# Rotary embedding: from half-batch slabs in nine slots to whole batches in five

## The chip, the core and the metric

The kernel runs on one core of a Trainium2 chip. The metric is the time of one execution on the device, in microseconds (us). Several runs are given by their median. A profile is one execution recorded by the hardware; its span runs from its first to its last instruction, and the time of the same execution lies a little above the span.

Five engines work side by side, each with its own order of instructions: TensorE (PE), VectorE (DVE), ScalarE (ACT), GpSimd (POOL) and SyncE (SP). Here SP issues all loads and ACT issues all stores. Sixteen DMA engines carry both. SBUF is the memory on the core, with 128 partitions; PSUM is the smaller one that TensorE writes to.

## The reference

```python
# x: (8, 2048, 8, 64) float32; cos, sin: (2048, 32) float32
x1 = x[..., :32]
x2 = x[..., 32:]
cos = cos[None, :, None, :]
sin = sin[None, :, None, :]
out1 = x1 * cos - x2 * sin
out2 = x1 * sin + x2 * cos
return np.concatenate([out1, out2], axis=-1)
```

Each row of x (one batch, one position, one head, 64 numbers) is rotated by the angle of its position. x is 33.55 MB, the output as much, each table 0.26 MB: for each number of x that is read and written there are two products and one addition.

## The kernel before

**Tiling.** The 2048 positions of a batch are split over 128 partitions, 16 consecutive ones each. So a partition holds 16 x 512 numbers of a batch: a row of 32 KB. The tables lie in the same way, 16 x 32 numbers (2 KB) per partition. A *slab* is half a batch, 8 positions per partition: 128 rows of 16 KB, 2 MB. There are 16 slabs, first the first halves of all batches, then the second halves. They live in `xpool`, nine slots of 16 KB per partition. The result is written over x in its slot, and stored from there.

**The three ways to rotate.** Work on a slab goes in tiles of 2048 numbers per partition (half a slab, 1 MB); the first slab begins and the last slab ends with smaller ones. `rotate` (from line 121) gives each tile one of three kinds. All three need a product t1 = x * cos and a product t2 = x * sin with the halves swapped, and their sum.

- Kind A, the usual one: GpSimd makes t2 in two instructions (L138, one for each half, the second with `nsin`, the negated table); VectorE makes t1 (L144) and adds (L151).
- Kind B: GpSimd makes t2 and VectorE t1, but TensorE adds them, by multiplying both with an identity matrix into the same PSUM bank (L156, L157), in four groups of 512 columns; ACT copies each group back over x (L158).
- Kind C: VectorE makes both products (L144, L161), TensorE adds them (L172, L173, with the negated identity `neye` for the first half), ACT copies (L176). GpSimd has nothing to do.

Slabs 5 and 10 are a C tile followed by a B tile; everything else is kind A.

**Buffers.** t1 of kind A lies in PSUM, in one slot. t2 of kinds A and B lies in `t2_pool`, three slots of 8 KB per partition. t1 of kinds B and C, and t2 of kind C, lie in `t1s_pool`, three slots of 8 KB under the one tag `t1s`. TensorE's sums go to `o_pool`, two PSUM banks. When a tile takes a slot that another one had, its first write waits until every reader of the earlier tile is done. Per partition SBUF holds 9 x 16 KB of slabs, 3 x 8 of `t1s`, 3 x 8 of `t2`, and 7 KB of tables and identities.

**Order.** `keep(...)` holds instructions of one engine in the order in which the program names them; VectorE's products and additions, ACT's evacuating copies and ACT's stores are held so. Stores run two slabs behind the computation (`LAG = 2`): after the tiles of slab i the kernel names the store of slab i - 2. The load of slab i + 6 is named after that; it takes the slot of slab i - 3 and waits for that slab's store. The last slab and the two before it are stored as early as they can be.

**Start.** ACT issues cos, SP issues 256 KB of x, then sin, then the rest of slab 0 in growing pieces (256 KB, 512 KB, 1 MB), then the slabs 1 to 8. ACT makes `nsin` from sin, then `neye`, and a copy of sin in PSUM; VectorE copies cos to PSUM (L108).

Of the kernel before, what the change touches and what calls it, by code (L numbers as in the profile page):

```python
# [9 lines left out]
@with_exitstack  # L10
def kernel(
    ctx: ExitStack,
    tc: tile.TileContext,
    x: bass.AP,
    cos: bass.AP,
    sin: bass.AP,
    out: bass.AP,
):
    nc = tc.nc
    keep = tc.keep_in_program_order  # L20
    f32 = mybir.dt.float32
    PSUM = bass.MemoryType.PSUM

    B, S, H, D = x.shape
    Dh = D // 2
    P = 128
    HD = H * D
    R = S // P

    SL = 8  # L30
    n_half = R // SL
    SLAB = SL * HD
    UNIT = 4 * HD
    NBUF = 9
    C = 512

    xv = x.rearrange("b (q r) h d -> b q (r h d)", q=P)
    ov = out.rearrange("b (q r) h d -> b q (r h d)", q=P)
    cos_src = cos.rearrange("(q r) d -> q r d", q=P)
    sin_src = sin.rearrange("(q r) d -> q r d", q=P)  # L40

    const_pool = ctx.enter_context(tc.tile_pool(name="const", bufs=1))
    tab_pool = ctx.enter_context(tc.tile_pool(name="tab", bufs=1, space=PSUM))
    t1_pool = ctx.enter_context(tc.tile_pool(name="t1p", bufs=1, space=PSUM))
    o_pool = ctx.enter_context(tc.tile_pool(name="op", bufs=2, space=PSUM))
    t1s_pool = ctx.enter_context(tc.tile_pool(name="t1s", bufs=3))
    xpool = ctx.enter_context(tc.tile_pool(name="xpool", bufs=NBUF))
    t2_pool = ctx.enter_context(tc.tile_pool(name="t2p", bufs=3))

    cos_sb = const_pool.tile([P, R, Dh], f32, tag="cb")  # L50
    sin_sb = const_pool.tile([P, R, Dh], f32, tag="sb")
    nsin = const_pool.tile([P, R, Dh], f32, tag="ns")
    eye = const_pool.tile([P, P], f32, tag="eye")
    neye = const_pool.tile([P, P], f32, tag="neye")
    cos_ps = tab_pool.tile([P, R, Dh], f32, tag="cp")
    sin_ps = tab_pool.tile([P, R, Dh], f32, tag="sp")

    slabs = [(b, l) for l in range(n_half) for b in range(B)]
    last = len(slabs) - 1
    xts = {}  # L60

    def cuts(i):
        if i == 0:
            return [HD, HD, 2 * HD, UNIT]
        return [SLAB]

    def pieces(i):
        if i == 0:
            return [HD, HD, 2 * HD, UNIT]
        if i == last:  # L70
            return [UNIT, 2 * HD, HD, HD]
        return [UNIT, UNIT]

    def spans(sizes):
        lo = 0
        for n in sizes:
            yield lo, n
            lo += n

    def load(i):  # L80
        b, l = slabs[i]
        xt = xpool.tile([P, SLAB], f32, tag="xt", name=f"xt{i}")
        for lo, n in spans(cuts(i)):
            nc.sync.dma_start(
                out=xt[:, lo : lo + n],
                in_=xv[b, :, l * SLAB + lo : l * SLAB + lo + n],
            )
            if i == 0 and lo == 0:
                nc.sync.dma_start(out=sin_sb, in_=sin_src)
        xts[i] = xt  # L90

    nc.scalar.dma_start(out=cos_sb, in_=cos_src)
    for i in range(NBUF):
        load(i)

    nc.gpsimd.memset(eye, 0.0)  # L96
    nc.gpsimd.affine_select(
        out=eye,
        in_=eye,
        compare_op=mybir.AluOpType.not_equal,  # L100
        fill=1.0,
        base=0,
        pattern=[[-1, P]],
        channel_multiplier=1,
    )
    nc.scalar.mul(nsin, sin_sb, -1.0)  # L106
    nc.scalar.mul(neye, eye, -1.0)
    nc.vector.tensor_copy(cos_ps, cos_sb)  # L108
    nc.scalar.copy(sin_ps, sin_sb)  # L109

    def rep(a, n):
        return dataclasses.replace(a, ap=[a.ap[0][:], a.ap[1][:], [0, n], a.ap[-1][:]])

    kinds = {}
    for i in (5, 10):
        kinds |= {(i, 0): "C", (i, UNIT): "B"}

    def rotate(i, lo, n):
        b, l = slabs[i]
        kind = kinds.get((i, lo), "A")  # L120
        xt = xts[i][:, lo : lo + n]
        r0 = l * SL + lo // HD
        nr = n // HD
        xk = xt.rearrange("p (r k d) -> p r k d", r=nr, d=Dh)
        xu = xt.rearrange("p (g u d) -> p g u d", u=2, d=Dh)
        if kind == "A":
            t1 = t1_pool.tile([P, n], f32, tag="t1")
        else:
            t1 = t1s_pool.tile([P, n], f32, tag="t1s")
        if kind == "C":  # L130
            t2 = t1s_pool.tile([P, n], f32, tag="t1s")
        else:
            t2 = t2_pool.tile([P, n], f32, tag="t2")
        t1u = t1.rearrange("p (g u d) -> p g u d", u=2, d=Dh)
        t2u = t2.rearrange("p (g u d) -> p g u d", u=2, d=Dh)
        if kind != "C":
            for u, tab in ((1, sin_sb), (0, nsin)):
                nc.gpsimd.tensor_mul(  # L138
                    out=t2u[:, :, u, :].rearrange("p (r h) d -> p r h d", h=H),
                    in0=xu[:, :, 1 - u, :].rearrange("p (r h) d -> p r h d", h=H),  # L140
                    in1=rep(tab[:, r0 : r0 + nr, :], H),
                )
        keep(
            nc.vector.tensor_mul(  # L144
                out=t1.rearrange("p (r k d) -> p r k d", r=nr, d=Dh),
                in0=xk,
                in1=rep(cos_ps[:, r0 : r0 + nr, :], 2 * H),
            )
        )
        if kind == "A":  # L150
            keep(nc.vector.tensor_add(out=xt, in0=t1, in1=t2))  # L151
        elif kind == "B":
            for j in range(n // C):
                o = o_pool.tile([P, C], f32, tag="o")
                cs = slice(j * C, (j + 1) * C)
                nc.tensor.matmul(o, eye, t1[:, cs], start=True, stop=False)  # L156
                nc.tensor.matmul(o, eye, t2[:, cs], start=False, stop=True)  # L157
                keep(nc.scalar.copy(xt[:, cs], o))  # L158
        else:
            keep(  # L160
                nc.vector.tensor_mul(  # L161
                    out=t2.rearrange("p (r k d) -> p r k d", r=nr, d=Dh),
                    in0=xk,
                    in1=rep(sin_ps[:, r0 : r0 + nr, :], 2 * H),
                )
            )
            G = C // Dh
            for u in range(2):
                for j in range(n // 2 // C):
                    o = o_pool.tile([P, C], f32, tag="o")  # L170
                    gs = slice(j * G, (j + 1) * G)
                    nc.tensor.matmul(o, eye, t1u[:, gs, u, :], start=True, stop=False)  # L172
                    nc.tensor.matmul(  # L173
                        o, eye if u else neye, t2u[:, gs, 1 - u, :], start=False, stop=True
                    )
                    keep(nc.scalar.copy(xu[:, gs, u, :], o.rearrange("p (g d) -> p g d", d=Dh)))  # L176

    LAG = 2

    def store(i, lo, n):  # L180
        b, l = slabs[i]
        keep(
            nc.scalar.dma_start(
                out=ov[b, :, l * SLAB + lo : l * SLAB + lo + n],
                in_=xts[i][:, lo : lo + n],
            )
        )

    for i in range(last + 1):
        if i == last:  # L190
            for k in range(i - LAG, i):
                store(k, 0, SLAB)
        for lo, n in spans(pieces(i)):
            rotate(i, lo, n)
            if i == last:
                store(i, lo, n)
        if LAG <= i < last:
            store(i - LAG, 0, SLAB)
        if i > LAG and i - LAG - 1 + NBUF <= last:
            load(i - LAG - 1 + NBUF)  # L200


# [28 lines left out]
```

## Time and profile before

| | |
|---|---|
| median of 3 runs | 164.71 us (164.56 to 164.76) |
| the profiled execution | 164.8 us |
| its span | 163.0 us |
| VectorE busy | 143.4 us (88%), 71 instructions |
| GpSimd busy | 139.4 us (86%), 74 instructions |
| TensorE busy | 33.3 us (20%) |
| ACT busy | 12.0 us (7%) |
| moved by the DMA engines | 67.66 MB |
| L144, tile of 2048 | 30 times, mean 2293 ns |
| L151, tile of 2048 | 26 times, mean 2292 ns |
| L138, 1024 (two per tile of 2048) | 56 times, mean 2336 ns |
| load of a slab, issue to landing | median 27.6 us |
| store of a slab, issue to landing | median 15.3 us |

In the lines of the profile an engine's name is followed by the line of the kernel, the operation, and output <- input. "x2" behind a line of the timeline means that so many instructions were merged. A bracket at the end gives the idle time of the engine just before, and what ended it. In the page's slices each digit stands for a fortieth of the span, 4.1 us, in tenths of busy time. A line of the windows gives, for a stretch of time, the busy time and count of PE, weight loads, DVE, ACT and POOL, then TensorE's granted clock as a share of full speed, the busy share of the DMA engines, and GB/s. A line of the waits names who waited for whom, the total in us, how often, and the longest.

### The profile page before, as it was taken

The numbers are of one execution on the slowest core, as the hardware profiler recorded it, in microseconds if no ns is written. First come the engines' busy times: TensorE is split into PE (matmuls) and PEld (weight loads), VectorE is DVE, ScalarE is ACT, GpSimd is POOL, SyncE is SP. The second block draws the span as 40 slices with busy tenths as digits, with TensorE's granted clock in tenths as the row PEclk, the third lists the DMA queues.
The fourth block names the chain that finished last, engine by engine and source line by source line (L and its number), as shares of the span: only waits on it lengthen the run. The fifth ranks groups of instructions, "written<-read, shape, count | busy, mean of one in ns | idle before, by whom it ended". The sixth has DMA issues, their size and how long they took to land. (4 is left out here: it accounts for less than half of the span.)

```text
span 163.0 us, 480 instructions
## 1 busy us (share of the span) xinstructions
PE 33.3 (20%) x64; PEld 13.4 (8%) x64; DVE 143.4 (88%) x71; ACT 12.0 (7%) x20; POOL 139.4 (86%) x74
## 2 busy tenths in 40 slices
PE   0000000000000079993000000899920000000000
PEld 0000000000000024440000000244400000000000
DVE  0587999999999999999899999999999999999900
ACT  3300000000000002232000000022410000000000
POOL 1599999999999999799999999956999999995000
PEclk9999999999999999999555555579997555555555
DMA  4999999999999999999999999999999999999995
GB/s 137 383 432 442 406 398 426 438 438 418 438 434 426 430 434 430 426 434 438 422 428 438 424 422 446 430 414 446 434 422 430 442 422 422 446 426 430 434 402 207
DMA packets 5763, 67.66 MB, mean 415 GB/s; under 512 B 640, under 2 KB 640, under 8 KB 1664
## 3 DMA queue, kind: packets, MB, share of 16 engines
q1 hardware_dynamic: 2880, 33.82, 49.5%
q10 hardware_dynamic: 2880, 33.82, 48.7%
q14 instruction: 3, 0.02, 0.0%
HBM read 34.08 MB, written 33.55 MB: 415 GB/s over the span
## 5 line engine op out<-in xcount | busy, mean ns | idle before, releaser
L138 POOL TENSOR_TENSOR t<-xt,sin_sb 128x1024 f32<-128x1024 f32 (+2 forms) x34 | 70.7, 2081 | 10.8 <-DVE xt L151 6.3
L144 DVE TENSOR_TENSOR t<-xt,cos_ps 128x2048 f32<-128x2048 f32 (+2 forms) x36 | 73.9, 2056 | 1.0
L138 POOL TENSOR_TENSOR t<-xt,nsin 128x1024 f32<-128x1024 f32 (+2 forms) x34 | 70.8, 2082 | 0.0
L151 DVE TENSOR_TENSOR xt<-t,t 128x2048 f32<-128x2048 f32 (+2 forms) x32 | 64.8, 2025 | 5.6 <-POOL t L138 2.1
L172 PE MATMUL o<-t,eye 128*128 128x512 f32 x16 | 11.3, 800 | 85.8 <-DVE t L144 85.8
L176 ACT COPY xt<-o 128x512 f32<-128x512 f32 x8 | 4.7, 586 | 94.5 <-DVE t L144 55.3
L172 PEld LDWEIGHTS o<-t,eye 128*128 128x128 f32 x16 | 3.9, 256 | 90.6 <-issue 90.6
L156 PE MATMUL o<-t,eye 128*128 128x512 f32 x16 | 8.2, 592 | 0.0
L157 PE MATMUL o<-t,eye 128*128 128x512 f32 x16 | 8.2, 592 | 0.0
L173 PE MATMUL o<-t,neye 128*128 128x512 f32 x8 | 6.2, 862 | 0.2 <-DVE t L161 0.2
L158 ACT COPY xt<-o 128x512 f32<-128x512 f32 x8 | 4.7, 586 | 9.0 <-PE o L157 9.0
L108 DVE COPY cos_ps<-cos_sb 128x512 f32<-128x512 f32 x1 | 0.7, 694 | 5.0 <-DMA cos_sb<-in_cos_dram 5.0
L161 DVE TENSOR_TENSOR t<-xt,sin_ps 128x2048 f32<-128x2048 f32 x2 | 4.6, 2281 | 0.0
L173 PE MATMUL o<-t,eye 128*128 128x512 f32 x8 | 4.1, 592 | 0.0
L157 PEld LDWEIGHTS o<-t,eye 128*128 128x128 f32 x16 | 3.0, 190 | 3.8 <-issue 3.8
L156 PEld LDWEIGHTS o<-t,eye 128*128 128x128 f32 x16 | 3.0, 190 | 3.8 <-issue 3.8
L173 PEld LDWEIGHTS o<-t,neye 128*128 128x128 f32 x8 | 2.0, 278 | 4.9 <-issue 3.3
L173 PEld LDWEIGHTS o<-t,eye 128*128 128x128 f32 x8 | 1.5, 190 | 1.9 <-issue 1.9
L106 ACT ACT_TABLE_LOAD x1 | 1.3, 1283 | 1.2 <-PEq L215 1.2
L106 ACT ACTIVATE nsin<-sin_sb 128x512 f32<-128x512 f32 x1 | 0.6, 630 | 3.2 <-DMA sin_sb<-in_sin_dram 3.2
L109 ACT COPY sin_ps<-sin_sb 128x512 f32<-128x512 f32 x1 | 0.6, 579 | 0.0
L96 POOL MEMSET eye<- 128x128 f32 x1 | 0.2, 205 | 0.3 <-POOLq L215 0.3
(6 smaller groups left out, 1.0 us busy)
## 6 DMA issues: line engine op xcount, KB each, us to landing
xt<-in_x_dram SPq DMA_DIRECT2D x15, 2048.0 KB, 27.6
out_dram<-xt ACTq DMA_DIRECT2D x15, 2048.0 KB, 15.3
xt<-in_x_dram SPq DMA_DIRECT2D x1, 1024.0 KB, 7.8
out_dram<-xt ACTq DMA_DIRECT2D x1, 1024.0 KB, 10.3
xt<-in_x_dram SPq DMA_DIRECT2D x2, 256.0 KB, 4.3
xt<-in_x_dram SPq DMA_DIRECT2D x1, 512.0 KB, 5.8
out_dram<-xt ACTq DMA_DIRECT2D x1, 512.0 KB, 8.9
out_dram<-xt ACTq DMA_DIRECT2D x2, 256.0 KB, 7.6
```

The lines of the kernel that those rows point to most:

```text
L106: nc.scalar.mul(nsin, sin_sb, -1.0)
L108: nc.vector.tensor_copy(cos_ps, cos_sb)
L138: nc.gpsimd.tensor_mul(out=t2u[:, :, u, :].rearrange("p (r h) d -> p r h d", h=H), in0=xu[:, :, 1 - u, :].rearrange("p (r h) d -> p r h d" ...
L144: nc.vector.tensor_mul(out=t1.rearrange("p (r k d) -> p r k d", r=nr, d=Dh), in0=xk, in1=rep(cos_ps[:, r0 : r0 + nr, :], 2 * H),)
L151: keep(nc.vector.tensor_add(out=xt, in0=t1, in1=t2))
L156: nc.tensor.matmul(o, eye, t1[:, cs], start=True, stop=False)
L157: nc.tensor.matmul(o, eye, t2[:, cs], start=False, stop=True)
L158: keep(nc.scalar.copy(xt[:, cs], o))
L161: nc.vector.tensor_mul(out=t2.rearrange("p (r k d) -> p r k d", r=nr, d=Dh), in0=xk, in1=rep(sin_ps[:, r0 : r0 + nr, :], 2 * H),)
L172: nc.tensor.matmul(o, eye, t1u[:, gs, u, :], start=True, stop=False)
L173: nc.tensor.matmul(o, eye if u else neye, t2u[:, gs, 1 - u, :], start=False, stop=True)
L176: keep(nc.scalar.copy(xu[:, gs, u, :], o.rearrange("p (g d) -> p g d", d=Dh)))
```

## The change

- Slabs are gone. A slot of `xpool` holds a whole batch, 128 rows of 32 KB, 4 MB; there are five slots (5 x 32 KB per partition). The eight batches are taken in order, in tiles of 2048 numbers as before: four per batch, the first batch beginning and the last batch ending with two tiles of 1024.
- `t1s_pool` has two slots instead of three.
- SP issues, in this order, the first 1 MB of x, cos, sin, the next 1 MB, the remaining 2 MB of batch 0, and then whole batches. ACT issues no load.
- Each batch is stored as soon as its tiles are named: one store of 4 MB, for the last batch 2 MB, 1 MB and 1 MB. The load of batch b + 5 is named right after the store of batch b.
- TensorE gets five tiles instead of four: batches 1 and 3 begin with a C tile and a B tile, batch 5 with a B tile.
- ACT makes the PSUM copy of sin before `neye`. The preparing instructions, the loads and GpSimd's products are now held in program order too.

```diff
-    NBUF = 9
+    NBUF = 5
...
-    t1s_pool = ctx.enter_context(tc.tile_pool(name="t1s", bufs=3))
+    t1s_pool = ctx.enter_context(tc.tile_pool(name="t1s", bufs=2))
...
+    def load(b):
+        xt = xpool.tile([P, ROW], f32, tag="xt", name=f"xt{b}")
+        for lo, n in spans([UNIT, UNIT, 2 * UNIT] if b == 0 else [ROW]):
+            keep(nc.sync.dma_start(out=xt[:, lo : lo + n], in_=xv[b, :, lo : lo + n]))
+            if b == 0 and lo == 0:
+                keep(nc.sync.dma_start(out=cos_sb, in_=cos_src))
+                keep(nc.sync.dma_start(out=sin_sb, in_=sin_src))
+        xts[b] = xt
+
+    def store(b, lo, n):
+        keep(nc.scalar.dma_start(out=ov[b, :, lo : lo + n], in_=xts[b][:, lo : lo + n]))
+
+    for b in range(NBUF):
+        load(b)
...
-    for i in (5, 10):
-        kinds |= {(i, 0): "C", (i, UNIT): "B"}
+    for b in (1, 3):
+        kinds |= {(b, 0): "C", (b, UNIT): "B"}
+    kinds[(5, 0)] = "B"
...
+    def pieces(b):
+        if b == 0:
+            return [2 * HD, 2 * HD, UNIT, UNIT, UNIT]
+        if b == last:
+            return [UNIT, UNIT, UNIT, 2 * HD, 2 * HD]
+        return [UNIT] * 4
+
+    for b in range(B):
+        done = 0
+        outs = list(spans([2 * UNIT, UNIT, UNIT] if b == last else [ROW]))
+        for lo, n in spans(pieces(b)):
+            rotate(b, lo, n)
+            done = lo + n
+            while outs and sum(outs[0]) <= done:
+                store(b, *outs.pop(0))
+        if b + NBUF <= last:
+            load(b + NBUF)
```

Here `HD` is 512 (one position), `UNIT` is 2048 and `ROW` 8192 numbers per partition. `rotate` itself is unchanged but for its indices and for `keep` around L138.

## The prediction

> **What bounds the kernel now.** I read the page's slices first, then the windows of the quiet stretches, then the timeline around the first pair of TensorE tiles, then the waits. All times in us from the start of the span, unless said otherwise.
>
> ```profile
> DVE  0587999999999999999899999999999999999900
> POOL 1599999999999999799999999956999999995000
> DMA  4999999999999999999999999999999999999995
> ```
>
> The DMA row is full from the second slice to the last but one, so the 16 DMA engines set the end. But VectorE (DVE) is full too, and stops two slices earlier. Two resources lie close together.
>
> ```profile
> 24.00:40.00 16.00, 0.00 (x0) 0.00 (x0) 15.48 (x8) 0.00 (x0) 16.00 (x8) 1.00 1.01 431
> 126.00:150.00 24.00, 0.00 (x0) 0.00 (x0) 23.24 (x11) 0.00 (x0) 22.12 (x13) 0.50 1.01 432
> ```
>
> These are two windows; the last number is GB/s. The engines move 431 GB/s with loads and stores mixed. 67.66 MB at 431 GB/s is 157.0. The last VectorE instruction ends at 154.29 + 0.69 = 155.0, the span at 163.0: 8 us of stores were still queued behind it. So VectorE could be some microseconds later before it counted, and not more.
>
> ```profile
> 57.73 2.28 DVE L161 TENSOR_TENSOR t<-xt,sin_ps 128x2048 f32<-128x2048 f32 x1
> 57.96 2.04 PE L172 MATMUL o<-t,eye 128*128 128x512 f32 x2 [57.96 <-DVE t L144]
> 59.93 4.49 DVE L144 TENSOR_TENSOR t<-xt,cos_ps 128x2048 f32<-128x2048 f32 x2
> 60.16 2.05 PE L173 MATMUL o<-t,neye 128*128 128x512 f32 x2 [0.15 <-DVE t L161]
> ...
> 66.04 1.02 PE L172 MATMUL o<-t,eye 128*128 128x512 f32 x2
> 66.90 1.02 PE L173 MATMUL o<-t,eye 128*128 128x512 f32 x2
> 67.76 1.02 PE L156 MATMUL o<-t,eye 128*128 128x512 f32 x2
> ```
>
> This timeline is what decides my forecast. A kind C tile writes both its products (L144, L161) into slots of `t1s`, and TensorE reads them in four groups, each an L172 and an L173. The last L172 runs from 66.04 to 67.06. VectorE has long gone on: at 59.93, right after L161, it writes the product of the kind B tile into the third slot of `t1s`.
>
> ```profile
> POOL t L138 <- DVE xt L151: 6.3, 3, 3.3
> SPq L84 <- DMA out_dram<-xt: 86.4, 7, 31.9
> ```
>
> The waits show that a writer waits until a slot's readers are done: GpSimd (POOL) for the additions that read its product (three slots), the sync queue for the stores that read an `xt` slot.
>
> **What the Trainium skill says.** "SBUF — State Buffer", section "SBUF size: 192, 224, or 256?", gives about 208 KiB usable per partition. The new kernel takes 5 x 32 for `xt`, 2 x 8 for `t1s`, 3 x 8 for `t2`, 7 for tables and identities: 207 KiB. So the third `t1s` slot has no room; no trace shows the limit itself. "DMA: Bandwidth & Descriptors", section "Queues, rings and completion order", says that an engine takes turns between the queues packet by packet. The trace agrees: with equal rows both ways the queues have 49.5% and 48.7%. I use equal shares below.
>
> **The change, part by part.**
>
> *Two slots in `t1s`.* Batches 1 and 3 begin with a C tile and then a B tile. C holds both slots; B's cosine product must wait for the last L172 (or for L173, 0.86 later). Everything on VectorE is kept in program order, so this wait holds the A tiles behind it too, although they need no `t1s` slot. From the lines above: without a wait B's product starts at 59.93, with it at 67.06 + 0.1 = 67.16: 7.2. At the second pair of the trace the product starts at 104.61 and the last L172 ends at 110.54 + 1.02 = 111.56: 7.05. I take 7.1 each, 14.2 together. Bounds: 6.9 and 8.0 (the L173) each. Below that is excluded as long as the wait is there, since no group can start before C's products are written. The store of the batch on the scalar queue, and the load five batches later behind that, wait too.
>
> *The start.* 1 MB of x and both tables now precede everything in one queue. Before, 0.53 MB moved in the first 4.0 us. The x has 8 KB rows, the tables 2 KB rows (the window 4 to 6, with 2 KB rows, gave 355 GB/s, 6 to 8 399). 1.57 MB then end at 4.0 + 1.04/0.40 = 6.6; before, about 0.85 passed from sin's last byte to its first use: 7.45, where GpSimd started at 5.74. Range 7.0 to 8.0. cos comes 0.65 earlier, so its copy (0.69) is done by 7.5.
>
> *Batch 0.* GpSimd sets it: two pieces of 1024 at 2 x 1.21, three of 2048 at 4.56 (instructions follow each other every 2.28): 7.45 + 4.85 + 13.7 = 26.0; the last addition, 2.3, ends at 28.3.
>
> *Batches 1 to 7 on VectorE.* An A tile takes 4.725 (additions start at 20.25, 24.98, 29.70); a C tile 4.4, a B tile 2.2 (starts at 55.53, 57.73, 59.93). Batches 1 and 3: 4.4 + 7.1 + 2.2 + 9.45 = 23.15. Batches 2, 4, 6: 18.9. Batch 5, with the fifth TensorE tile alone and `t1s` free: 2.2 + 14.2 = 16.4. Batch 7: three A tiles, 14.2, and two halves at 2.6 (149.37 to 151.97): 19.4. Ends: 51.5, 70.4, 93.5, 112.4, 128.8, 147.7, 167.1.
>
> *Does anything else hold it longer?* Loads: read alone till 29.8 (first byte about 2.8), 11.6 MB; then half the rate beside stores. Batch 1 has landed at 24, batch 2 at 41, batch 3 at 60, 4 at 73; load 5 needs store 0 finished (49.5) and lands about 93, load 6 at 109, load 7 at 129. VectorE wants them at 112, 129 and 148. So whole-batch loads cost nothing here, because of the waits; without these see the first rival. GpSimd fills its three `t2` slots during a wait and then keeps ahead at 4.56 a tile; B's slot is read until 6.9 after B's product, which brings the next product exactly in time (0 to 0.5 lost each). ACT evacuates as before and issues store 0 before the C tile's copies: 0.
>
> *The end.* The last store is 1 MB, issued at 167.1 with nothing left in the queues, as a store comes every 4.7 and takes 2.4. Fixed part: the last store of before was issued at 155.0 and took 7.6; after 155 the windows still moved 0.43 + 0.80 + 0.80 + 0.42 = 2.45 MB, 5.7 at 431 GB/s, leaving 1.9 ("DMA: Bandwidth & Descriptors", section "Anatomy of one DMA — SWDGE (gpsimd) path", has about 2.0 for another kind of queue). 1.05/0.431 + 1.9 = 4.35: 171.5. Before, 163.0 - 162.6 = 0.4 followed: a span of about 171.9. Bounds of the tail: 3.7 to 5.5.
>
> *Larger rows, fewer DMAs.* 16 KB rows already give 431 GB/s. If 32 KB rows give up to 1% more, 1.6 us of DMA time is saved; here that is hidden, for VectorE is last.
>
> Sum: 163.0 + 8.9 = 171.9. The profiled run took 164.8, 1.8 more than its span, and lies 0.1 over the median of 164.71. 171.9 + 1.8 - 0.1 = **173.6**.
>
> **Rivals.** *First, the other side: the wait is absent and the DMA engines set the end, 163.6.* Its place is B's product in batches 1 and 3; its price is the DMA engines' own time. Without the 14.2 the work of VectorE would end at 152.9, and then loads hold it: batch 7 would land at 135 (half rate from 29.8 on), so 156.6. The DMA engines need 2.9 + 157.0 + 1.6 = 161.5, and 0.4: a span of 161.9. That saves the slow small rows at both ends and the hole of the window 20 to 22 (319 GB/s). For it: the full DMA row, and 32 KB rows can't be worse than 16 KB by anything seen. Against it: C holds both slots. It decides from this point: the tail behind VectorE is 4.8, so the span stays below 163.0 while VectorE ends before 158.2, that is while the two waits cost under 5.3 together. I work out 14.2. Chance 0.06.
>
> *Second: only one wait counts, 166.5.* If batch 3 came late from HBM, its wait would run in time that VectorE lost anyway. Against it: batch 3 lands at 60 and VectorE reaches it at 70. Chance 0.03.
>
> *Third: the throttle stretches the wait, about 181.* The granted clock falls to 0.5 in the page's slices; were the second C tile's groups at half rate, its wait would be 7 longer. Against it: at a mean clock of 0.81 in the window 100 to 120 the ACT copies still come every 1.72, as in the first pair. Chance 0.04.
>
> **How the numbers follow.** Forecast 0.87, rivals 0.06, 0.03, 0.04. The parts' bounds (waits -0.4 to +1.8, start and batch 0 -0.5 to +0.6, tail -0.6 to +1.1, GpSimd 0 to 1) add up, not all one way, to 171.8 to 176.0; this holds over 9 tenths of the forecast, so about 8 in 10 of all. 0.2% is about what a measurement can tell from no change. Faster: most of the first rival, 0.05; the rest 0.01 within. Slower: 0.94.
>
> **What would show it.** Right: VectorE idle about 7 before L144 in batches 1 and 3, released by L172 of TensorE; no DVE wait on a load after batch 0; batch 0 done near 28; the DMA row no longer full towards the end; VectorE's last end near 167, span near 172. Wrong: DVE busy through both pairs, or waiting on loads of batches 4 to 7, and a DMA row full to the end: then it is the first rival. A first use of the tables far from 7.5, or an A tile other than 4.7, would show a wrong term and move the sum by as much.

## The result, and the profile after

The changed kernel takes 173.55 us (median of 4 runs, 173.02 to 173.9) against 164.72 us before (164.56 to 164.76): a ratio of 1.0535, 95% interval 1.0501 to 1.057. The forecast was 173.6. The profiled execution took 173.02, its span is 171.0.

First the rows of the page's slices for the changed kernel that answer to those of the kernel before. A slice is now 4.3 us.

```profile
DVE  0477999607999999940999999999999999999980
POOL 1399999992099999994049999999999999999700
DMA  5999999999999999999999999999999990598955
```

VectorE has two holes, at slices 8 and 9 and at 18 and 19, where the row before had none. GpSimd has a hole of its own just behind each. The DMA row has its holes somewhere else: it stays full through both of VectorE's and falls to 0 some 60 us after the second.

The chain of work that ended last, by engine:

```profile
DVE 63%; DMA 17%; PE 8%; POOL 6%; issue 3%; SPq 0%; DVEq 0%; ACTq 0%; POOLq 0%
```

Read as shares of the span: the chain runs through VectorE almost from the start, and TensorE (PE) stands in it with 8%. TensorE is busy for a quarter of the span and far from full; it is in the chain only because something on VectorE waited for it. Where, the timeline of VectorE shows. (In the changed kernel the products are L129 for cosine and L146 for sine, the addition is L136, and the matmuls of kind C are L157 and L158.)

```profile
28.27 2.28 DVE L129 TENSOR_TENSOR t<-xt,cos_ps 128x2048 f32<-128x2048 f32 x1
30.47 2.28 DVE L146 TENSOR_TENSOR t<-xt,sin_ps 128x2048 f32<-128x2048 f32 x1
39.69 4.49 DVE L129 TENSOR_TENSOR t<-xt,cos_ps 128x2048 f32<-128x2048 f32 x2 [6.94 <-PE o L157]
44.29 2.29 DVE L136 TENSOR_TENSOR xt<-t,t 128x2048 f32<-128x2048 f32 x1
```

The two products of batch 1's C tile follow each other at 2.20. The next row merges B's product and the first product of the A tile behind it, and its bracket is the new wait: VectorE stood still for 6.94 us, until a matmul of L157 was done. The second pair, from the timeline of both engines:

```profile
72.31 2.28 DVE L146 TENSOR_TENSOR t<-xt,sin_ps 128x2048 f32<-128x2048 f32 x1
...
80.00 1.02 PE L157 MATMUL o<-t,eye 128*128 128x512 f32 x2
80.86 1.02 PE L158 MATMUL o<-t,eye 128*128 128x512 f32 x2
81.06 4.49 DVE L129 TENSOR_TENSOR t<-xt,cos_ps 128x2048 f32<-128x2048 f32 x2 [6.47 <-PE o L157]
```

The last L157 runs from 80.00 to 81.02, and B's product starts at 81.06. It does not wait for the last L158, which starts at 80.86 and is still running. So the slot that B takes is the one of C's cosine product, and it is free as soon as the last reader of that product is done.

At the other end, the windows of the changed kernel (columns as before, the last one GB/s):

```profile
134.00:140.00 6.00, 0.00 (x0) 0.00 (x0) 5.76 (x4) 0.00 (x0) 6.00 (x3) 0.50 1.00 431
140.00:142.00 2.00, 0.00 (x0) 0.00 (x0) 2.00 (x1) 0.00 (x0) 2.00 (x2) 0.50 0.42 180
142.00:146.00 4.00, 0.00 (x0) 0.00 (x0) 3.86 (x3) 0.00 (x0) 4.00 (x3) 0.50 0.00 0
```

Here the price is paid. From 142 to 146 the DMA engines have nothing left: every load has landed, every finished batch is stored, and VectorE is still working on batch 6. Before, VectorE had been ahead and stores were queued behind it until the end.

### The profile page after: what moved, and what is told of

The parts are those of the page before. It is cut to its first block, busy times and chain, and to the rows that moved or that the text cites. A ratio compares the mean times of both kernels' runs of the same rounds, so it can differ in the third digit from the quotient of the medians.

```text
span 171.0 us, 462 instructions
## 1 busy us (share of the span) xinstructions
PE 42.1 (25%) x80; PEld 16.7 (10%) x80; DVE 140.5 (82%) x66; ACT 14.3 (8%) x24; POOL 138.6 (81%) x70
## 2 busy tenths in 40 slices
DMA packets 3170, 67.65 MB, mean 396 GB/s; under 512 B 352, under 2 KB 352, under 8 KB 608
## 4 chain that ended last, share of the span: by engine, by line
DVE 63%; DMA 17%; PE 8%; POOL 6%; issue 3%; SPq 0%; DVEq 0%; ACTq 0%; POOLq 0%
DVE t L129 32%; DVE xt L136 28%; DMA out_dram<-xt 14%; POOL t L122 6%; PE o L158 4%; PE o L157 3%; DMA sin_sb<-in_sin_dram 3%; DVE t L146 3%; DVEq L136 0%; SPq L69 0%; SPq L67 0%; ACTq L74 0%; POOLq L122 0%
## 5 line engine op out<-in xcount | busy, mean ns | idle before, releaser
L122 POOL TENSOR_TENSOR t<-xt,sin_sb 128x1024 f32<-128x1024 f32 (+1 forms) x32 | 70.7, 2211 | 22.4 <-DVE xt L136 16.5
L129 DVE TENSOR_TENSOR t<-xt,cos_ps 128x2048 f32<-128x2048 f32 (+1 forms) x34 | 73.4, 2168 | 14.3 <-PE o L157 13.4
L122 POOL TENSOR_TENSOR t<-xt,nsin 128x1024 f32<-128x1024 f32 (+1 forms) x32 | 70.8, 2211 | 0.0
L136 DVE TENSOR_TENSOR xt<-t,t 128x2048 f32<-128x2048 f32 (+1 forms) x29 | 62.2, 2145 | 5.0 <-POOL t L122 2.2
L157 PE MATMUL o<-t,eye 128*128 128x512 f32 x16 | 10.7, 760 | 54.0 <-DVE t L129 54.0
L141 PE MATMUL o<-t,eye 128*128 128x512 f32 x24 | 13.5, 646 | 26.5 <-DVE t L129 26.5
L142 PE MATMUL o<-t,eye 128*128 128x512 f32 x24 | 13.2, 632 | 0.0
L143 ACT COPY xt<-o 128x512 f32<-128x512 f32 x12 | 7.0, 585 | 42.6 <-PE o L142 42.6
L162 ACT COPY xt<-o 128x512 f32<-128x512 f32 x8 | 4.7, 586 | 60.8 <-PE o L158 60.8
L157 PEld LDWEIGHTS o<-t,eye 128*128 128x128 f32 x16 | 3.8, 251 | 58.8 <-POOL t L122 30.7
L141 PEld LDWEIGHTS o<-t,eye 128*128 128x128 f32 x24 | 4.7, 209 | 33.8 <-issue 29.0
L158 PE MATMUL o<-t,neye 128*128 128x512 f32 x8 | 6.2, 864 | 0.2 <-DVE t L146 0.2
L142 PEld LDWEIGHTS o<-t,eye 128*128 128x128 f32 x24 | 4.9, 203 | 6.3 <-issue 6.3
L146 DVE TENSOR_TENSOR t<-xt,sin_ps 128x2048 f32<-128x2048 f32 x2 | 4.6, 2281 | 0.0
L158 PE MATMUL o<-t,eye 128*128 128x512 f32 x8 | 4.1, 593 | 0.0
L158 PEld LDWEIGHTS o<-t,neye 128*128 128x128 f32 x8 | 1.8, 256 | 4.6 <-issue 2.9
L158 PEld LDWEIGHTS o<-t,eye 128*128 128x128 f32 x8 | 1.5, 190 | 1.9 <-issue 1.9
```

Of the source, the lines that this page charges most:

```text
L122: nc.gpsimd.tensor_mul(out=t2u[:, :, u, :].rearrange("p (r h) d -> p r h d", h=H), in0=xu[:, :, 1 - u, :].rearrange("p (r h) d -> p r h d" ...
L129: nc.vector.tensor_mul(out=t1.rearrange("p (r k d) -> p r k d", r=nr, d=Dh), in0=xk, in1=rep(cos_ps[:, r0 : r0 + nr, :], 2 * H),)
L146: nc.vector.tensor_mul(out=t2.rearrange("p (r k d) -> p r k d", r=nr, d=Dh), in0=xk, in1=rep(sin_ps[:, r0 : r0 + nr, :], 2 * H),)
L158: nc.tensor.matmul(o, eye if u else neye, t2u[:, gs, 1 - u, :], start=False, stop=True)
```

## The experiments

All are timed against the kernel before on the same chip. The first four ask whether the slots of `t1s` make the time, or the coarse batches: one puts the slots alone into the old kernel, one takes the wait away from the new one, one takes half of it away, and one trades it for another wait. The rest ask what sets the end once the wait is gone, and where the 0.6% come from by which the kernel without the wait is faster than the one before.

### 1. The slots alone, in the old kernel

```diff
-    t1s_pool = ctx.enter_context(tc.tile_pool(name="t1s", bufs=3))
+    t1s_pool = ctx.enter_context(tc.tile_pool(name="t1s", bufs=2))
```

> The kernel before with one edit: two t1s slots instead of three. Slot theory: B's cosine product of slabs 5 and 10 waits for the last group of the C tile before it, about 6.9 us each time, twice; VectorE then ends near 155.0 + 13.8 = 168.8, and with the fixed 1.9, the last 256 KB (0.6) and 0.4 behind it the span is about 171.7, the time about 173.5. Rival (whole batches are too coarse: the time is lost by 4 MB loads and stores): nothing of that is in this kernel, so 164.7.

Measured: 172.77, ratio 1.0483 (1.044 to 1.0525). Its waits of VectorE:

```profile
DVE t L144 <- PE o L172: 12.9, 2, 6.5
DVE xt L151 <- POOL t L138: 2.1, 3, 1.0
```

This is the old kernel with its 2 MB slabs, and it loses 8.0 us by one number. Its span is 171.1, as long as that of the changed kernel to 0.1. The second line is the same as before the change. The last VectorE instruction ends at 167.38 + 0.69 = 168.07, 13.1 later than before, which is the 12.9 of the two waits to within 0.2. Whole batches can't be the cause here, for there are none.

### 2. Both pairs apart

Between C and B come the two A tiles of the batch; slots, batches and the number of tiles stay.

```diff
-        kinds |= {(b, 0): "C", (b, UNIT): "B"}
+        kinds |= {(b, 0): "C", (b, 3 * UNIT): "B"}
```

> The changed kernel with the C tile at the head and the B tile at the end of batches 1 and 3, two A tiles between them, so that TensorE is done with C before B's product is due; two slots, whole batches, five tiles stay. Slot theory: no VectorE wait on TensorE; the DMA engines set the end, the first rival's sum: 163.6 (162.5 to 165). VectorE starts to wait for loads from batch 4 on. Coarse-batch rival: still about 173.

Measured: 163.82, ratio 0.9936 (0.9921 to 0.9951): 9.7 us faster than the changed kernel, and 0.6% faster than the one before. The slices:

```profile
DVE  0468899999999999999999999999999999999500
DMA  5999999989999999999999999999999999999995
```

VectorE has no hole, and the DMA row is full to the last slice again. VectorE ends at 151.17 + 1.22 = 152.39, and 9.7 us of stores follow. The time was right, but VectorE's waits for loads, which the expectation named, did not come. Batch 7 was in its slot at 129.4 and not at 135. The sum behind 135 gives the loads half the rate from 29.8 on. In the trace stores move nothing before 32, and again nothing from 52 to 56: store 0 landed at 53.2, and store 1 was issued only at 53.9, because B's evacuation by TensorE and ACT now stands at the end of batch 1. In these 4 us the loads moved 1.74 MB, 0.9 more than at half the rate, which is worth about 4 us to the loads behind. After batch 3 there is no such gap: when store 3 was issued, at 88.3, store 2 was still under way (to 96.5).

### 3. One pair apart

```diff
-    for b in (1, 3):
-        kinds |= {(b, 0): "C", (b, UNIT): "B"}
+    for b, at in ((1, 3 * UNIT), (3, UNIT)):
+        kinds |= {(b, 0): "C", (b, at): "B"}
```

> As the last, but only batch 1 has its pair apart; batch 3 keeps C and B side by side. Slot theory: one wait of about 6.5 is left, VectorE ends near 166.2 - 6.9 = 159.3, then the tail of 4.8: a span near 164.1, time about 166 (165.5 to 167.5). If the two waits do not add (one of them hidden behind late loads), 173 or 163.6. Coarse-batch rival: 173.

Measured: 166.54, ratio 1.0102 (1.007 to 1.0134).

```profile
DVE t L129 <- PE o L157: 6.3, 1, 6.3
```

One wait left, 6.3. From two waits to one the time falls by 7.0; from one to none only by 2.7, because then the DMA engines are last. That bend is what the point of decision in the first rival describes. In the profiled runs VectorE ends at 152.39 without a wait, at 159.21 with one and at 166.16 with two, so 6.8 and 13.8 later, and the span grows by 2.0 and 8.9: some 5 us are free each time, and the rest comes out whole. (The medians, 2.7 and 9.7 above the kernel without a wait, leave a little less free; the kernels with a wait spread more from run to run.)

### 4. Another slot for C's sine product

C's sine product moves to the pool of `t2`, so B finds a free `t1s` slot with the pair side by side.

```diff
-            t2 = t1s_pool.tile([P, n], f32, tag="t1s")
+            t2 = t2_pool.tile([P, n], f32, tag="t2")
```

> The changed kernel with the pair side by side, but C's sine product takes a slot of the t2 pool (three slots) instead of t1s, so that B's cosine product finds a free t1s slot. Slot theory: the wait of VectorE on TensorE before B's product goes; but C now holds a t2 slot until TensorE's fourth group, so GpSimd's second A product of the batch comes later and VectorE's addition waits about 2.6 in each of the two batches. VectorE ends near 166.2 - 2 x (6.7 - 2.6) = 158.0, time near 164.8 (163.6 to 166.5). Coarse-batch rival: 173.

Measured: 168.06, ratio 1.019 (1.0175 to 1.0206), above the expected range. VectorE's waits:

```profile
DVE xt L136 <- POOL t L122: 11.4, 6, 2.4
```

The wait on TensorE is gone, as expected, and additions wait for GpSimd instead. The changed kernel has 2.2 of this in all, at the start; so 9.2 are new, not the 5.2 that I had put in. The expectation counted one addition in each of batches 1 and 3. The timeline shows four: at 44.17 in batch 1, at 81.33 and 88.33 in batch 3, and at 111.18 in batch 5, waits of 2.43, 2.45, 2.38 and 1.98. GpSimd itself had stood still before the first three, by 4.71, 5.04 and 2.40, until the addition of an A tile was done and it had a slot of `t2`. That used its lead up. It needs 4.56 for an A tile and VectorE 4.72, so it wins back only 0.16 a tile, and the B tile of batch 5, which takes VectorE 2.2, finds it late once more. Taking the place from `t2` buys back 5.5 of the 8.8 us lost; moving the tiles apart, which costs nothing, buys back all of them and 0.9 more.

### 5. The fifth tile, with the pairs apart and side by side

In both kernels the line that makes batch 5's first tile kind B is left out:

```diff
-    kinds[(5, 0)] = "B"
```

> The kernel with both pairs apart, without the fifth TensorE tile: batch 5 begins with a kind A tile. VectorE has one addition more and ends near 152.4 + 2.5 = 154.9; with the tail of 4.8 that makes 159.7, less than the span of 162.1 which the DMA engines set: no change, 163.8. If VectorE set the end here too: 166.3.

Measured with the pairs apart: 163.82, ratio 0.9937 (0.9921 to 0.9953): no change, though VectorE ends at 154.9, 2.5 later.

> The changed kernel with its pairs side by side, without the fifth TensorE tile. Slot theory: VectorE sets the end here, so the one addition more in batch 5 (2.3, and 0.1 of gaps) comes out whole: 173.55 + 2.4 = 175.9 (175 to 176.5), where the same edit did nothing with the pairs apart. If the DMA engines set the end of the changed kernel: no change, 173.5.

Measured with the pairs side by side: 175.07, ratio 1.0621 (1.0589 to 1.0654), which is 1.5 above the changed kernel's median, with runs from 174.38 to 175.78. The expectation was met at its lower edge. So the same edit counts where VectorE is last and is hidden where the DMA engines are.

### 6. A tail without 8 KB rows

```diff
-        outs = list(spans([2 * UNIT, UNIT, UNIT] if b == last else [ROW]))
+        outs = list(spans([2 * UNIT] * 2 if b == last else [ROW]))
```

> The kernel with both pairs apart, the last batch stored as 2 MB and 2 MB instead of 2, 1 and 1 MB, so that no store has 8 KB rows. The windows from 148 to 160, with stores alone, show about 409 GB/s against 426 to 436 before them; if 8 KB rows are the reason, the last 2 MB take 0.2 us less: 163.6. If stores alone are slower whatever their rows: 163.8, no change.

Measured: 163.91, ratio 0.9943 (0.9926 to 0.9959); no difference from experiment 2 can be told, so the 0.2 us that 8 KB rows might have cost are not seen.

### 7. Where the 0.9 us over the kernel before come from

With the wait gone, the new order is a little faster than the old kernel. I took it for the start, since 296 GB/s in the first 8 us stand against 255. Two experiments ask. One keeps everything of experiment 2 and cuts each whole-batch load and store into two:

```diff
-        for lo, n in spans([UNIT, UNIT, 2 * UNIT] if b == 0 else [ROW]):
+        for lo, n in spans([UNIT, UNIT, 2 * UNIT] if b == 0 else [ROW // 2] * 2):
...
-        outs = list(spans([2 * UNIT, UNIT, UNIT] if b == last else [ROW]))
+        outs = list(spans([2 * UNIT, UNIT, UNIT] if b == last else [ROW // 2] * 2))
...
-            while outs and sum(outs[0]) <= done:
+            while outs and sum(outs[0]) <= done and (b == last or done == ROW):
```

> The kernel with both pairs apart, every whole-batch load and store cut in two DMAs of 2 MB with 16 KB rows, issued at the same points. Theory that the gain over the kernel before comes from the start alone: the same as with 32 KB rows, 163.8 within 0.3. Theory that larger rows move faster: 1% of 157 us at most, so up to 165.4.

Measured: 164.74, ratio 0.9997 (0.9988 to 1.0006). The gain is gone. The other gives the old kernel the new start:

```diff
     def cuts(i):
         if i == 0:
-            return [HD, HD, 2 * HD, UNIT]
+            return [UNIT, UNIT]
...
     def pieces(i):
         if i == 0:
-            return [HD, HD, 2 * HD, UNIT]
+            return [2 * HD, 2 * HD, UNIT]
...
             if i == 0 and lo == 0:
+                nc.sync.dma_start(out=cos_sb, in_=cos_src)
                 nc.sync.dma_start(out=sin_sb, in_=sin_src)
...
-    nc.scalar.dma_start(out=cos_sb, in_=cos_src)
```

> The kernel before with only the order of the first loads changed: 1 MB of x, cos and sin on the sync queue, then the rest, and slab 0 in tiles of 1024, 1024 and 2048. Theory that the gain of the kernel with pairs apart over the kernel before comes from the start (0.33 MB more moved in the first 8 us, 0.77 us): 163.9. VectorE starts about 2 us later and ends near 156.5, with 2.9 of tail below the DMA engines' end. Theory that it comes from whole batches or their rows: 164.7.

Measured: 165.34, ratio 1.0042 (1.0026 to 1.0058): no gain, rather a loss. Its windows, and then those of the kernel before:

```profile
0.00:8.00 8.00, 0.00 (x0) 0.00 (x0) 1.76 (x2) 2.04 (x4) 1.34 (x7) 1.00 0.78 293
20.00:40.00 20.00, 0.00 (x0) 0.00 (x0) 19.45 (x9) 0.00 (x0) 20.00 (x10) 1.00 1.00 407
```

```profile
0.00:8.00 8.00, 0.00 (x0) 0.00 (x0) 2.18 (x4) 2.63 (x4) 2.96 (x10) 1.00 0.75 255
20.00:40.00 20.00, 0.00 (x0) 0.00 (x0) 19.34 (x10) 0.00 (x0) 20.00 (x10) 1.00 1.00 420
```

The new start moves 0.30 MB more in the first 8 us, and 0.26 MB less from 20 to 40. In the five kernels whose windows I read closely the rate falls for some microseconds after 20; here the dip is deeper (213 GB/s at 23, where the kernel before has nothing under 295). Why it is there, and why it grows, stays open.

So my explanation by the start fell, and the last run asks whether the length of the pieces counts or the number of DMAs. It keeps the 4 MB DMAs of experiment 2 and puts a gap of 32 bytes into the middle of each partition of a slot:

```diff
-        xt = xpool.tile([P, ROW], f32, tag="xt", name=f"xt{b}")
+        xt = xpool.tile([P, 2, HALF + 8], f32, tag="xt", name=f"xt{b}")
```

> The kernel with both pairs apart and 4 MB loads and stores as there, but with a gap of 32 bytes in the middle of each partition of a slot, so that the memory of a 4 MB DMA falls into pieces of 16 KB while the number of DMAs, their size and all points of issue stay. If the length of the pieces makes the 0.9 us between 32 KB rows (163.8) and 16 KB rows in twice as many DMAs (164.7): 164.7. If the number or size of the DMAs makes it: 163.8.

Measured: 164.48, ratio 0.9982 (0.9974 to 0.999), between the two. The page counts 4962 packets for it, 3170 for experiment 2 and 5187 for the one with two DMAs. Of the 0.0061 between 0.9936 and 0.9997, 0.0046 come with the shorter pieces and 0.0015 with the greater number of DMAs; the first is clear of the noise, the second barely, since the two intervals touch. The windows from 40 to 140 go the same way: with 32 KB rows, with the gap, and with two DMAs (three kernels, one line each).

```profile
40.00:140.00 100.00, 37.59 (x64) 15.04 (x64) 97.55 (x43) 9.82 (x17) 97.14 (x43) 0.69 1.00 433
```

```profile
40.00:140.00 100.00, 39.96 (x67) 15.72 (x65) 96.58 (x43) 10.07 (x18) 96.25 (x43) 0.67 1.01 432
```

```profile
40.00:140.00 100.00, 39.53 (x66) 15.48 (x64) 97.17 (x43) 9.97 (x17) 96.75 (x43) 0.65 1.01 430
```

## Why the prediction was right, point by point

The mechanism and its size were right. Around it several terms were off, and the misses cancelled; that the sum came out within 0.1 is luck.

- **The wait in the two slots.** The mechanism is shown from both sides: it appears with two slots in the old kernel (+8.0 us) and goes with the order in the new one (-9.7). Its size was 7.1 each; the delay of B's product measured 39.69 - (28.27 + 4.4) = 7.0 and 81.06 - (70.12 + 4.4) = 6.5. That the slot is freed by L157 and not L158, which I left open as a bound of 8.0, is settled by the second pair above.
- **The start and batch 0.** The tables were used from 7.1 on (7.45 was taken): 0.70 MB had moved in the first 4.0 us, where the prediction took the 0.53 of the kernel before. Batch 0 ended at 28.36 (28.3), but GpSimd did not set it: its last product was done at 25.7, and the last two additions, at 21.34 and 26.07, waited for nothing on GpSimd. VectorE, at 4.73 a tile, was last. The earlier start and the other limit cancelled.
- **The ends of the batches on VectorE.** Predicted 51.5, 70.4, 93.5, 112.4, 128.8, 147.7, 167.1; measured 51.3, 70.2, 92.7, 111.6, 127.8, 146.8, 166.16. Of the 0.9 that the sum was too long, 0.6 are the two waits; the rest is spread over the pieces.
- **Loads not in the way.** Loads 5, 6 and 7 landed at 93.4, 110.5 and 129.9 (93, 109, 129), each 17 to 18 us before VectorE reached it. The sum used equal shares of the two queues, derived from the Trainium skill, "DMA: Bandwidth & Descriptors", section "Queues, rings and completion order", where an engine takes turns between the queues packet by packet. The 49.5% and 48.7% that the prediction sets beside it can't show this, for each queue moves 33.8 MB whatever the turns; the trace before shows it from 30 to 50, where the two queues moved 4.31 and 4.29 MB. That the landings were met to 1.5 us is in part luck: store 0 landed at 53.0 and not at 49.5, so load 5 was issued later, and from 50 to 70 the loads moved 5.14 MB against 3.41 of the stores.
- **GpSimd.** It waited 7.2 and 9.3 us for `t2` slots and did not hold VectorE up afterwards. I had allowed 0 to 0.5 each; it was 0. The prediction has it wait for B's slot. But its next products started at 46.66 and 88.03, each 0.08 after the addition of the first A tile behind B, while TensorE was reading B's product until 49.23 and 90.60.
- **The tail.** From VectorE's last end to the end of the span 4.84; 4.8 was taken. Its two parts were wrong. The prediction took 7.6 for the last store of the kernel before, which is the median of its two 256 KB stores; the one issued at 155.0 took 7.2. So 1.5 and not 1.9 is the fixed part, and 0.8 and not 0.4 followed; the sum of the two is the same. In the changed kernel the last store took 3.8, which is 1.4 more than its bytes at 431 GB/s, and 1.0 followed. The closeness of 1.9 to the figure for the other kind of queue came from that reading.
- **Sum.** 171.0 for the span of the profiled run, against 171.9; two of the four runs have 171.9. The median of the four spans is 171.55, and their times lie 2.0 above them, where the prediction added 1.7. These two misses cancel as well.
- **The first rival.** Its point of decision held: one wait left costs time, none does not. Its time of 163.6 was met by experiment 2 (163.82), with one of its reasons wrong (VectorE's waits for batch 7) and one not borne out (the gain at the start: experiment 7 keeps the new start and gains nothing). The third rival's half rate of TensorE did not come, though the clock that it feared did: from 72.5 to 77, in the first groups of the second C tile, the granted clock was 0.54, and the wait was 6.47, against 6.94 for the first C tile at a clock of 1.00.
- **32 KB rows.** "Up to 1% more" was put down as hidden. No run takes them out of the changed kernel, where VectorE is last; without the wait, whole rows and fewer DMAs are worth 0.6%.

## What to carry to other kernels

Before a pool loses a slot, write down who holds the slots when the next tile asks for one, until which reader, and what stands behind the asking instruction on its engine: here 8 KB per partition saved in a pool of scratch tiles cost 13.4 us on VectorE, in a kernel whose page shows the DMA engines full from end to end. Where there is no memory for the third slot, distance does the same work as a slot: two tiles moved apart in the order of the batch removed the wait at no cost. And an engine that ends 8 us before the span, beside a full resource, has less than that in hand: 3.0 us (old kernel) to 4.8 us (new) of stores still follow its last instruction when it comes last. Up to about 5 us of new waits stayed unseen here, and everything beyond came out whole.

## What the runs showed that I had not expected

The wait on TensorE is not one number. For the same four groups VectorE stood still for 6.94 and 6.47 in the changed kernel, 7.2 and 6.6 in the one without the fifth tile, 6.3 where one wait is left, and 6.5 and 6.4 in the old kernel with two slots. Most of the difference lies in the second group after TensorE has been idle: its L157 pair takes 1.48 in batch 1 of the changed kernel and 1.07 in batch 3, and the later pairs take 1.02 in both. This would fit the spread between runs: 0.9 to 1.6 in the four kernels with a wait (4 to 6 runs each), 0.3 to 0.5 in the new kernels without one and with as few runs. But the kernel before has 0.9 over 35 runs, and the old kernel with the new start 1.9 over 22, without any wait. Why the second group differs, and what makes the spread, stays open.
